# New landing times, DMA rates and matmul steps in the recorder that orders a two-layer GLA and differential-attention trunk

## The chip, the core and the metric

The kernel runs on one core of a Trainium2 chip. Each engine works through its own queue of instructions in order: PE (matmuls, with its weight loads shown as PEld), DVE and ACT (element-wise work), POOL (GpSimd) and SP, whose queue here issues all DMAs. The metric is device time in microseconds (us) of one execution; smaller is better.

## The reference

Two layers over 2048 tokens of width 1024, float32. Each layer normalises and modulates its input, makes one combined projection (width 3600), runs two groups of heads on it, and projects the result back into the residual:

```python
h = rms_norm(x, norm_g[l]) * (1.0 + scale) + shift        # scale, shift, gate from c @ w_ada
gq, gk, gv, glr, gz, dq, dk, dv, dz = split_columns(h @ w_in[l])
# group A, 4 heads: gated linear attention by chunks of 64, state read at the chunk's end
# group B, 4 heads: differential attention, two softmax maps of dh 64, values of 128
p = softmax(where(key_chunk <= query_chunk, q @ k.T, -inf))
attn = p[map 0] - lam * p[map 1]
o_diff = rms_norm(attn @ v) * (1 - lam_init) * silu(dz)
x = x + gate * (concat(o_gla, o_diff) @ w_out[l])
```

## The kernel before

The tokens are worked on in four units of 512 (`u` = 0 to 3), in both layers (`l`). Dense projections are split into a high and a low part in fp32r, three 512-wide matmuls for each 128x128 block (`acc<-w,hhi`, `acc<-w,hlo`, and `oh`, `ol` for the output projection). Weights split in this way are kept in DRAM (`wd`) and loaded again for later units into four buffers `w` of 512 KB.

Attention of a unit and head works by query tiles of 128 (`qt`). For each of the two maps, matmuls make the scores (`sc<-Kj,qh` and `ql`, `Kj` from earlier units and `Kt` from this one); DVE takes the running minimum of the negated scores while it copies them into a score tile `s`, ACT takes the exponential. There are five `s` tiles. POOL first fills a corner of each new one with a mask value (`MEMSET s`). DVE then makes the difference of the two maps. The product with the values needs the weights turned. For most heads (88 query tiles in all, called turned) this goes partly through DRAM: DVE transposes 32x32 blocks (`turn_blocks`), a DMA writes them (`ad<-s`), another reads them back in turned order by pieces of 64 elements (`s<-ad`), and the product `po<-Vj,s` reads that; the tile's own unit is turned on PE (`tp<-ident,s`) and comes in through `po<-Vt,s`. After the product ACT sums squares, POOL takes a power (`wq`), DVE scales by it and the gate (`z`), and PE transposes `z` for the output projection (`to_oT`).

Nothing is issued as it is written. Python generators (`run_streams`) for attention, GLA, dense work and so on take turns by a virtual clock; each instruction is recorded by `Program.record` with its cost (`Program.cost`), its dependencies and its buffers. In `pv`, `WAIT` is how much later on that clock, beyond the arithmetic, the product of a turned query tile may be recorded. `Program.order` then lists the instructions anew: engine by engine, it picks the recorded instruction that is ready, with the lowest turn, by its own table of costs and of latencies from one engine to another (`LAT`; row `S` is the landing of a DMA as seen by ACT, DVE, POOL, PE and another DMA). For the DMA queue it counts 1150 ns from the issue, bytes by a rate, and at most eight in flight. `best_order` repeats that sixty times with changed turns and keeps the order with the shortest span by its own table. `issue` puts the instructions out in that order from one line, which is why the profile shows all work at L370. The table decides only the order; on the chip each engine waits on semaphores.

Of the kernel before, what the change touches and what calls it, by code (L numbers as in the profile page):

```python
# [22 lines left out]
P = 128  # L23
# [97 lines left out]
class Program:  # L121
# [2 lines left out]

    LAT = {"A": dict(A=142, V=141, G=159, T=260, S=84), "V": dict(A=128, V=127, G=155, T=202, S=20),
           "G": dict(A=150, V=100, G=340, T=203, S=17), "T": dict(A=197, V=196, G=200, T=0, S=200),
           "S": dict(A=930, V=930, G=1650, T=1300, S=1700)}

    def __init__(self, **engines):
        self.ops = []  # L130
# [44 lines left out]
    @staticmethod  # L175
    def cost(e, method, args, kw, out):
        n = math.prod(out.shape[1:])
        if e == "S":
            return math.prod(out.shape) * 4 / (256.0 if out.shape[-1] == 64 else 360.0)
        if e == "T":  # L180
            if method == "transpose":
                return 110
            rate = {F32R: 2.4, BF16: 2.4, F32: 0.6}[args[2].dt]
            if rate == 0.6 and args[1].shape[1] < P:
                return 54 if args[1].shape[0] == CH else 60
            return max(n * 0.444, 112 * args[1].shape[1] / P) if rate == 2.4 else max(n / rate, 216) + 6
        ins = [a for a in list(args[1:]) + list(kw.values()) if isinstance(a, View) and a is not kw.get("accum_out")]
        scalars = sum(math.prod(a.shape[1:]) == 1 for a in ins) if n > 1 else 0
        psum = any(a.buf.psum for a in ins)
        half = 112 if out.shape[0] <= 64 and n > 16 else 0  # L190
        if method == "tensor_reduce":
            n = math.prod(ins[0].shape[1:])
        if e == "A":
            return 0.834 * n + (45 if psum else 85) + 93 * (scalars + ("accum_out" in kw)) + half
        if e == "G":
            return 300 + 165 * n if kw.get("op") == ALU.pow else 100 + 2.2 * n
        fast = method in ("tensor_copy", "tensor_scalar") and not psum
        return (0.52 if fast else 1.042) * n + 70 + 61 * scalars + half + 30 * ("accum_out" in kw)
# [175 lines left out]
def trunk_kernel(ctx, tc, x, c, w_ada, b_ada, norm_g, w_in, conv_w, w_gk, b_gk, gla_norm_g,  # L374
# [3 lines left out]
    S = x.shape[1]  # L378
# [22 lines left out]
    V, A, G, T, SY = (prog.queue(e) for e in "VAGTS")  # L401
# [210 lines left out]
    def pe(cost, wait=0.0):  # L612
        return ("pe", cost, wait)
# [434 lines left out]
        HD[key, hd, "q"] = (qh, ql, Kt, Vt, sz)  # L1048
        done("qkT", key, hd)

    WAIT, AFTER = 7.0, 0.0

    def attn_gen(l, u, hd):
        y = layers[l]
# [321 lines left out]
```

## Time and profile before

| | |
|---|---|
| time, median of 3 runs | 2473.82 us (2470.57 to 2479.25) |
| the profiled execution | 2474.07 us, span 2472.4 us |
| instructions | 39660 |
| PE busy | 2408.5 us, 97% |
| DVE, ACT, POOL busy | 1778.4, 1289.0, 138.2 us |
| DMA moved | 568.33 MB, mean 230 GB/s |
| mean granted PE clock | 0.997 |

A profile row names an engine, an operation and its tiles as out<-in, without the numbers of buffers; a wait is put down to what ended it.

### The profile page before, as it was taken

The page shows a single profiled execution, that of the slowest core. Times are in us where ns is not written, and L with a number is a line of the kernel's source. Part 1 is how long each engine was busy: PE and PEld are TensorE (multiplying, and loading weights), DVE is VectorE, ACT ScalarE, POOL GpSimd, SP SyncE. Part 2 cuts the span into 40 slices and gives each one's busy share as a digit, 9 for nine tenths or more (in the row PEclk, how much of TensorE's full clock was granted, in tenths as well). Part 3 has the DMA queues.
Part 4 walks back from the last instruction along what each step waited for, and adds up shares of the span by engine and source line. Part 5 has one row for each costly group of instructions (what it writes and reads, how often), then busy time and mean ns, then how long its engine had stood idle before and what let it go on. Part 6 is the DMA issues. An engine that isn't in the chain of part 4 may idle for free.

```text
span 2472.4 us, 39660 instructions
## 1 busy us (share of the span) xinstructions
PE 2408.5 (97%) x13251; PEld 1962.4 (79%) x13251; DVE 1778.4 (72%) x5169; ACT 1289.0 (52%) x2912; POOL 138.2 (6%) x424
## 2 busy tenths in 40 slices
PE   7999999999999999899999999999999999999999
PEld 5887777787888878787788877888888887878887
DVE  4879777882878828688864895668728887287883
ACT  5757544562555624454773574456614566144552
POOL 0001000010000000000000010000000000000000
PEclk9999999999999999999999999999999999999999
DMA  8777887676686866678457867676677777676763
GB/s 266 275 245 273 310 275 237 215 254 213 216 249 193 278 227 193 195 223 228 143 208 272 283 251 276 207 231 204 201 250 233 229 224 238 213 221 184 233 200 129
DMA packets 425996, 568.33 MB, mean 230 GB/s; under 512 B 195968, under 2 KB 300608, under 8 KB 425792
## 3 DMA queue, kind: packets, MB, share of 16 engines
q1 hardware_dynamic: 425792, 565.79, 70.7%
q8 instruction: 105, 1.72, 0.3%
q14 instruction: 99, 0.81, 0.1%
HBM read 410.52 MB, written 161.48 MB: 231 GB/s over the span
## 4 chain that ended last, share of the span: by engine, by line
PE 43%; DMA 4%; DVE 4%; ACT 1%; issue 1%; SPq 0%; POOL 0%; POOLq 0%; DVEq 0%; ACTq 0%
PE acc L370 29%; PE sc L370 6%; PE po L370 5%; PE tp L370 3%; DVE s L370 2%; DMA ad<-s 2%; DMA s<-ad 1%; DMA w<-wd 1%; SPq L370 0%; DMA wr<-in_w_ada_dram 0%; ACT s L370 0%; DMA xt<-xd 0%; POOL wq L370 0%; DVE w L370 0%; DVE z L370 0%
## 5 line engine op out<-in xcount | busy, mean ns | idle before, releaser
L370 PE MATMUL acc<-w,hhi 128*128 128x512 f32 x2560 | 836.1, 401 | 5.4 <-DMA w<-wd 3.5
L370 PEld LDWEIGHTS acc<-w,hhi 128*128 128x128 f32 x2560 | 466.3, 189 | 97.6 <-DMA w<-wd 7.0
L370 PE MATMUL acc<-w,hlo 128*128 128x512 f32 x1280 | 506.4, 396 | 0.0
L370 ACT ACTIVATE s<-s,mx 128x512 f32<-128x512 f32 (+15 forms) x256 | 308.0, 1204 | 249.6 <-DVE s L370 145.6
L370 PE MATMUL acc<-hhi,w 128*128 128x512 f32 x1024 | 352.1, 398 | 1.4 <-DVE z L370 1.4
L370 PE MATMUL acc<-w,oh 128*128 128x512 f32 x1024 | 333.6, 400 | 3.7 <-ACT oh L370 1.6
L370 DVE TENSOR_SCALAR_CACHE_REDUCE s<-sc,mx 64x64 f32<-64x64 f32 (+5 forms) x640 | 307.1, 483 | 31.1 <-PE sc L370 12.9
L370 PEld LDWEIGHTS acc<-w,hlo 128*128 128x128 f32 x1280 | 240.9, 188 | 49.0 <-issue 1.3
L370 PEld LDWEIGHTS acc<-w,oh 128*128 128x128 f32 x1024 | 189.2, 189 | 44.7 <-DVE t L370 3.6
L370 PEld LDWEIGHTS acc<-hhi,w 128*128 128x128 f32 x1024 | 191.8, 188 | 39.4 <-PE tp L370 1.9
L370 PE MATMUL po<-Vj,s 128*128 128x128 f32 x1536 | 201.7, 283 | 12.7 <-DMA s<-ad 11.4
L370 PEld LDWEIGHTS po<-Vj,s 128*128 128x128 f32 x1536 | 193.4, 197 | 23.9 <-DMA s<-ad 17.8
L370 PE MATMUL acc<-w,ol 128*128 128x512 f32 x512 | 202.3, 398 | 0.0
L370 PE MATMUL acc<-hlo,w 128*128 128x512 f32 x512 | 201.1, 393 | 0.0
L370 DVE SCALAR_TENSOR_TENSOR s<-s,r 128x512 f32<-128x512 f32 (+2 forms) x320 | 198.5, 666 | 2.5
L370 DVE TENSOR_SCALAR_CACHE_REDUCE s<-sc 128x512 f32<-128x512 f32 (+4 forms) x256 | 158.5, 621 | 42.6 <-PE sc L370 38.1
L370 ACT COPY rw<-acc 128x256 f32<-128x256 f32 x128 | 48.0, 375 | 237.2 <-PE acc L370 236.9
L370 PE MATMUL sc<-Kj,qh 128*128 128x512 f32 x384 | 160.4, 418 | 1.0 <-DVE ol L370 0.6
L370 POOL MEMSET s<- 64x64 f32 x256 | 38.5, 151 | 2058.1 <-PE po L370 1384.7
L370 PE MATMUL sc<-Kj,ql 128*128 128x512 f32 x384 | 153.0, 398 | 0.0
L370 ACT CAST w<-raw 128x512 fp32r<-128x512 f32 x152 | 93.2, 626 | 109.0 <-PE acc L370 92.7
L370 DVE TENSOR_TENSOR w<-raw,w 128x512 fp32r<-128x512 f32 x152 | 103.3, 686 | 61.0 <-ACT w L370 60.1
(185 smaller groups left out, 3738.3 us busy)
## 6 DMA issues: line engine op xcount, KB each, us to landing
w<-wd SPq DMA_DIRECT2D x424, 512.0 KB, 4.4
wd<-w SPq DMA_DIRECT2D x144, 512.0 KB, 4.0
raw<-in_w_in_dram SPq DMA_DIRECT2D x120, 256.0 KB, 4.6
Kj<-kd SPq DMA_DIRECT2D x48, 512.0 KB, 5.7
ad<-s SPq DMA_DIRECT2D x24, 768.0 KB, 4.7
s<-ad SPq DMA_DIRECT2D x24, 768.0 KB, 5.9
wr<-in_w_ada_dram SPq DMA_DIRECT2D x128, 128.0 KB, 3.6
ad<-s SPq DMA_DIRECT2D x32, 512.0 KB, 3.7
```

What stands on the lines that cost most here:

```text
L370: getattr(self.engines[e], method)(*[real(a) for a in args], **{k: real(v) for k, v in kw.items()})
```

## The change

Three places of numbers are changed; no instruction is added or left out. The landing of a DMA (row `S` of `LAT`) counts 250 to 700 ns more. The DMA rate, in bytes per ns, is now taken by the size of the last dimension: 208 instead of 256 for 64, 326 instead of 360 for 256, 350 instead of 360 for all others. The steps of matmuls are 0.4485 ns an element instead of 0.444 in fp32r, and 8 or 18 ns of surcharge instead of 6 in float32, the larger one where the stationary operand is a view of more than one step. `WAIT` is 9.0 instead of 7.0.

```diff
-           "S": dict(A=930, V=930, G=1650, T=1300, S=1700)}
+           "S": dict(A=1500, V=1500, G=1900, T=2000, S=2200)}
...
         if e == "S":
-            return math.prod(out.shape) * 4 / (256.0 if out.shape[-1] == 64 else 360.0)
+            return math.prod(out.shape) * 4 / {64: 208.0, 256: 326.0}.get(out.shape[-1], 350.0)
...
-            return max(n * 0.444, 112 * args[1].shape[1] / P) if rate == 2.4 else max(n / rate, 216) + 6
+            if rate == 0.6:
+                return max(n / rate, 216) + (18 if len(args[1].path) > 1 else 8)
+            return max(n * 0.4485, 112 * args[1].shape[1] / P)
...
-    WAIT, AFTER = 7.0, 0.0
+    WAIT, AFTER = 9.0, 0.0
```

The order moves on every engine, mostly by a few places. Three places follow.

On PE in layer 0, fourth unit, first head, ahead of the product of the third query tile (`s_9812` is the tile that comes back from DRAM, `hhi` and `hlo` the input of a projection, `rw` and `z` are other heads' transposes). Before:

```order
L370 MATMUL acc_10531<-w_10597,hhi_9578 128x512 x2
L370 MATMUL acc_10531<-w_10597,hlo_9595 128x512
L370 MATMUL tp_10819<-ident_101,z_10141 128x128 x2
L370 MATMUL tp_10828<-ident_101,s_10567 128x128 x4
L370 MATMUL po_10839<-Vt_10134,s_10724 128x128 x4
L370 MATMUL po_10787<-Vj_9114,s_9812 128x128 x4
L370 MATMUL po_10787<-Vj_9717,s_9812 128x128 x4
L370 MATMUL po_10787<-Vj_9800,s_9812 128x128 x4
```

Now, with that tile as `s_9837`:

```order
L372 MATMUL po_10842<-Vt_10133,s_10699 128x128 x3
L372 MATMUL acc_10859<-w_10758,hhi_9343 128x512 x2
L372 MATMUL acc_10859<-w_10758,hlo_9355 128x512
L372 MATMUL acc_10859<-w_10763,hhi_9348 128x512 x2
L372 MATMUL acc_10859<-w_10763,hlo_9363 128x512
L372 MATMUL acc_10877<-w_10758,hhi_9343 128x512 x2
L372 MATMUL acc_10877<-w_10758,hlo_9355 128x512
L372 MATMUL acc_10877<-w_10763,hhi_9348 128x512 x2
L372 MATMUL acc_10877<-w_10763,hlo_9363 128x512
L372 MATMUL po_10760<-Vj_9130,s_9837 128x128 x4
L372 MATMUL po_10760<-Vj_9768,s_9837 128x128 x4
```

Before, ten short matmuls stood between the last projection matmul and the product; now the tile's own part (`Vt`) is earlier, and twelve projection matmuls follow it.

On SP, the round trip of the same query tile (`ad3_2` in DRAM, `kd` and `vp` keys and values of earlier units). Before:

```order
L370 DMA Kj_10691<-kd0_1_1355 128x1024
L370 DMA w_10698<-wd0_2_1_1776 128x1024
L370 DMA Kj_10711<-kd1_1_4778 128x1024
L370 DMA Kj_10717<-kd2_1_7836 128x1024
L370 DMA ad3_2_10777<-s_10528 128x6x256
L370 DMA w_10805<-wd0_2_2_1833 128x1024
L370 DMA w_10814<-wd0_2_3_1855 128x1024
L370 DMA s_9812<-ad3_2_10777 128x24x64
L370 DMA Vj_10846<-vp0_1_1253 128x512
L370 DMA ad3_3_10851<-s_10724 128x6x256
L370 DMA s_10567<-ad3_3_10851 128x24x64
```

Now:

```order
L372 DMA Kj_10679<-kd0_1_1355 128x1024
L372 DMA Kj_10702<-kd1_1_4776 128x1024
L372 DMA Kj_10727<-kd2_1_7801 128x1024
L372 DMA ad3_2_10753<-s_10517 128x6x256
L372 DMA w_10758<-wd0_2_0_1770 128x1024
L372 DMA w_10763<-wd0_2_1_1776 128x1024
L372 DMA s_9837<-ad3_2_10753 128x24x64
L372 DMA w_10815<-wd0_2_2_1832 128x1024
L372 DMA w_10825<-wd0_2_3_1855 128x1024
L372 DMA ad3_3_10855<-s_10699 128x6x256
L372 DMA Vj_10864<-vp0_1_1252 128x512
```

The write stands two weight loads earlier in the queue: those of the first two pieces of the next item now follow it.

On PE at the end of that unit, where the transposes of `z` wait for the third query tile of the third head (`s_11748` before, `s_11751` now). Before:

```order
L370 MATMUL po_12274<-Vj_11741,s_11748 128x128 x4
L370 MATMUL acc_12237<-w_12310,hhi_9499 128x512
L370 MATMUL acc_12237<-w_12310,hlo_9524 128x512
L370 MATMUL acc_12265<-w_12299,hhi_9494 128x512 x2
L370 MATMUL acc_12265<-w_12299,hlo_9507 128x512
L370 MATMUL tp_12439<-ident_101,z_11186 128x128 x2
L370 MATMUL sc_12445<-Kj_12215,qh_12349 128x512
L370 MATMUL sc_12445<-Kj_12215,ql_12383 128x512
L370 MATMUL acc_12265<-w_12310,hhi_9499 128x512 x2
L370 MATMUL acc_12265<-w_12310,hlo_9524 128x512
L370 MATMUL acc_12286<-w_12299,hhi_9494 128x512 x2
L370 MATMUL tp_12439<-ident_101,z_11186 128x128
```

Now:

```order
L372 MATMUL acc_12083<-w_12316,hhi_9465 128x512 x2
L372 MATMUL acc_12083<-w_12316,hlo_9477 128x512
L372 MATMUL acc_12231<-w_12306,hhi_9457 128x512 x2
L372 MATMUL acc_12231<-w_12306,hlo_9472 128x512
L372 MATMUL acc_12231<-w_12316,hhi_9465 128x512 x2
L372 MATMUL acc_12231<-w_12316,hlo_9477 128x512
L372 MATMUL acc_12267<-w_12306,hhi_9457 128x512 x2
L372 MATMUL acc_12267<-w_12306,hlo_9472 128x512
L372 MATMUL acc_12267<-w_12316,hhi_9465 128x512 x2
L372 MATMUL acc_12267<-w_12316,hlo_9477 128x512
L372 MATMUL tp_12449<-ident_101,z_11190 128x128 x3
```

Before, two of the transposes stood ahead of the third, with twelve 512-wide matmuls between the product and the last; now all three stand together, behind eighteen, of which the rows show fifteen.

## Prediction

> **What bounds the kernel now.** I read the page first, then the waits of PE, the timeline of PE and of the DMA-issuing queue around the longest waits, and the granted clock in stretches around them. The page's first lines:
>
> ```profile
> span 2472.4 us, 39660 instructions
> PE 2408.5 (97%) x13251; PEld 1962.4 (79%) x13251; DVE 1778.4 (72%) x5169; ACT 1289.0 (52%) x2912; POOL 138.2 (6%) x424
> ```
>
> PE is busy for all but 2472.4 - 2408.5 = 63.9 us. No instruction is added or removed by the change, so what PE must do stays; what an order can win lies in those 63.9 us, and in the time that matmuls run at a lower clock. PE's waits, largest first (engine and tile that waited, what ended the wait, us in total, times, longest us):
>
> ```profile
> PE po L370 <- DMA s<-ad: 11.4, 10, 4.8
> PE tp L370 <- DVE z L370: 8.1, 8, 4.0
> PE tp L370 <- DMA wr<-in_w_ada_dram: 5.3, 3, 4.0
> PE tp L370 <- DVE s L370: 4.0, 6, 2.1
> PE acc L370 <- DMA w<-wd: 3.5, 4, 2.0
> ```
>
> The largest is the one that the change speaks of: the attention product (po) waits for the second half of the round trip through DRAM (s<-ad) that turns the attention weights. The fifth is the load of the projections' weights. The third lies at the very start, before there is other work, and the order of the first thirty DMA issues is nearly the same in both orders: it stays. The longest wait of all, in the timeline of PE (start, busy us, what, idle before it and its releaser):
>
> ```profile
> 980.65 0.34 PE L370 MATMUL sc<-Kt,ql 128*128 128x384 f32 x1
> ...
> 1000.45 1.16 PE L370 MATMUL po<-Vt,s 128*128 128x128 f32 x8 [0.67 <-ACT s L370]
> 1006.44 4.42 PE L370 MATMUL po<-Vj,s 128*128 128x128 f32 x24 [4.83 <-DMA s<-ad]
> ```
>
> The query tile's last score matmul starts at 980.65, and its product at 1006.44. Between them the queue that issues the DMAs did this:
>
> ```profile
> 994.54 0.37 SPq L370 DMA_DIRECT2D ad<-s  x1
> 997.49 1.01 SPq L370 DMA_DIRECT2D w<-wd  x2
> 998.61 0.37 SPq L370 DMA_DIRECT2D s<-ad  x1
> 1001.64 2.90 SPq L370 DMA_DIRECT2D Vj<-vp  x1
> ```
>
> The read was issued at 998.61 and released PE at about 1006.4, some 7.8 us later. The typical times from issue to landing, and what the granted clock did in 10 us around the long waits (PE, PEld, DVE, ACT, POOL busy, clock, DMA share, GB/s):
>
> ```profile
> w<-wd SPq DMA_DIRECT2D x424, 512.0 KB, 4.4
> ad<-s SPq DMA_DIRECT2D x24, 768.0 KB, 4.7
> s<-ad SPq DMA_DIRECT2D x24, 768.0 KB, 5.9
> ```
>
> ```profile
> 1002.00:1012.00 10.00, 5.05 (x29) 4.81 (x30) 5.15 (x20) 1.10 (x5) 0.59 (x3) 0.83 0.84 221
> 1165.00:1175.00 10.00, 5.96 (x21) 4.49 (x21) 5.29 (x15) 1.24 (x2) 1.53 (x4) 0.83 0.76 213
> 1202.00:1212.00 10.00, 8.09 (x33) 4.99 (x32) 8.69 (x23) 4.50 (x10) 1.76 (x4) 0.83 0.75 265
> 2189.00:2199.00 10.00, 8.03 (x33) 6.34 (x32) 9.64 (x26) 3.34 (x5) 0.00 (x0) 0.83 1.11 303
> 2437.00:2447.00 10.00, 8.28 (x41) 6.61 (x39) 3.23 (x6) 1.94 (x5) 0.55 (x1) 0.83 0.23 81
> 2216.00:2226.00 10.00, 7.45 (x49) 6.44 (x48) 7.58 (x27) 2.71 (x11) 0.70 (x3) 1.00 0.84 245
> ```
>
> Five stretches have a clock of 0.83, so each loses 0.17 x 10 = 1.7 us of matmul time on top of its idle time; 8.5 us in all.
>
> **The change, part by part.** The recorder's table says when it believes a DMA has landed; it never made PE wait, semaphores do. The old table, for a 768 KB read of 64-element pieces: 1.15 us of issue, 786432 B / 256 = 3.07 us, 1.30 us to PE, 5.5 us in all, against the 5.9 us of the row. The new one: 1.15 + 786432 / 208 = 3.78 + 2.00 = 6.9 us. For the weights, 524288 / 360 = 1.46 gave 3.9 us against 4.4 us, and now 1.50 + 3.15 = 4.6 us. So the old one promised data about half a microsecond early, the new one late by 1.0 and 0.2 us. The matmul steps are the smaller edit: 0.444 x 512 = 227 ns becomes 230 ns, and this row has
>
> ```profile
> 1792.00:1854.00 62.00, 62.00 (x282) 51.39 (x281) 18.09 (x55) 11.96 (x29) 0.00 (x0) 1.00 0.71 249
> ```
>
> 62 us / 282 = 220 ns for a mixture with shorter ones; a step 1% longer in the table moves nothing by itself, and I price it at nothing, with no cover at stake. WAIT 9 instead of 7 lets attention's product stand 2 us later in the order's starting point. In the order as built, I counted for each of the 88 turned query tiles the PE instructions between the tile's last score matmul and its product, each 512-wide matmul at 0.23 us and the others at their own steps: 19.3 us on average before, 21.2 us now. I call this the cover. Now term by term.
>
> *The waits for s<-ad, 11.4 us.* Of the ten, these four have the rows that matter (with the one above):
>
> ```profile
> 2219.11 0.62 PE L370 MATMUL po<-Vj,s 128*128 128x128 f32 x3 [1.71 <-DMA s<-ad]
> 2231.56 0.62 PE L370 MATMUL po<-Vj,s 128*128 128x128 f32 x3 [0.33 <-DMA s<-ad]
> 2266.15 0.62 PE L370 MATMUL po<-Vj,s 128*128 128x128 f32 x3 [0.59 <-DMA s<-ad]
> 444.02 0.74 PE L370 MATMUL po<-Vj,s 128*128 128x128 f32 x4 [1.24 <-DMA s<-ad]
> 494.23 0.62 PE L370 MATMUL po<-Vj,s 128*128 128x128 f32 x3 [0.92 <-DMA s<-ad]
> ```
>
> At 1006.44 the cover has 37 projection matmuls before and 65 now: 28 x 0.23 = 6.4 us more, against a wait of 4.83. At 2219 it is 45 and 66, 4.8 us more against 1.71; at 2231 and 2266 it grows by 6.6 and 7.1 us. These four, 4.83 + 1.71 + 0.33 + 0.59 = 7.5 us, go. At 444 the cover grows by 1.0 (0.2 us stays); at 494 it shrinks by 1.5 (0.92 becomes 2.4); the other four small ones change by little. So the six others keep their 3.9 us. Two query tiles whose products started without any wait lose cover:
>
> ```profile
> 1611.59 0.62 PE L370 MATMUL po<-Vj,s 128*128 128x128 f32 x3
> 2053.25 0.62 PE L370 MATMUL po<-Vj,s 128*128 128x128 f32 x4
> ```
>
> They lose 2.5 and 3.4 us. If their DMAs are issued as late as before, that is up to 5.4 us of new waits (the second has some half a microsecond to spare); if the order issues them earlier too, as the later landings in its table demand, nothing. I take half, 2.7. The term: -7.5 + 2.7 = -4.8 us, bounds -11.4 and +1.
>
> *The weights, 3.5 us in four waits*, of which one is most:
>
> ```profile
> 2192.45 0.51 PE L370 MATMUL acc<-w,hhi 128*128 128x512 f32 x1 [1.97 <-DMA w<-wd]
> ```
>
> PE work from the release of the buffer to the first use: 2.7 us before, 4.2 now, so 1.97 becomes 0.5; the three others gain 1.8 to 3.9 us of cover and go. But ten loads now have under 5.5 us, where six had. -2.5 us, bounds -3.5 and 0.
>
> *A wait on DVE that is a DMA's.* The 4.04 us of the second row:
>
> ```profile
> 1169.49 0.33 PE L370 MATMUL tp<-ident,z 128*128 128x128 f32 x1 [4.04 <-DVE z L370]
> ```
>
> ```profile
> 1167.58 0.14 POOL L370 MEMSET s<- 64x64 f32 x1 [5.29 <-DMA ad<-s]
> ```
>
> The chain: POOL's queue held a memset of a score tile until the write ad<-s had left its buffer, and behind it on POOL stood the power (wq) that DVE's z needs, which PE transposes. Cover from the product to the transposes: 3.1 us before, 5.4 now (the third place of the order above). 2.1 us go, 1.9 stay, since on POOL a memset that waits for a DMA still stands ahead of the power. Bounds -4.0 and 0.
>
> *The clock.* Of five slow stretches, those of 1006 and 2192 rest on waits that go: 2 x 1.7 = 3.4 us, bounds 0 and -5.1. Rows first: the stretch of 2189 lost its clock after a single idle time of 1.97 us, and that of 2216 with 1.71 us did not. The Trainium skill, TensorE: Matmul & The Clock Gate, section "HAM oscillation — how this bites in real kernels", has the rule that idle gaps over about 3.4 us are to be avoided. By that rule only the gaps of 4.83 and 4.04 us would cost clock here, and the term would be 1.7 us; the rows show more stretches than that, so the rows decide.
>
> *All other waits* (63.9 - 11.4 - 3.5 - 4.0 = 45 us, the start's included) rest on durations that the change leaves alone. Their covers move both ways: 2.1 us more at one transpose of scores, 1.5 to 2 us less at some first score matmuls. 0, bounds -6 and +6.
>
> The sum: -4.8 - 2.5 - 2.1 - 3.4 = -12.8 us. The profiled execution took 2474.07 us (1.7 us around its span), and the median of the runs shown is 2473.82: the same. 2474 - 13 = 2461.
>
> **The rivals.** *Waits move, none go (about 2470).* The table has one landing time whatever else is in flight. In the 2189 row DMA stands at 303 GB/s and a share of 1.11; at 1001.64 one issue took the queue 2.90 us. If a late landing is a matter of load, then a fixed 0.7 us more helps the median, not the ten worst: at 1006.44 the read took 7.8 us, over the new table's 6.9 too. Then only the four big covers count, 7.5 us, and new waits of 5.4 us stand against them, with one slow stretch gone: 2474 - 7.5 + 5.4 - 1.7 = 2470. For it: the covers lost above. Against it: the ones gained are larger than any landing seen. The Trainium skill, DMA: Bandwidth & Descriptors, section "Latency and other measured facts", says that HBM access takes 0.2 us on average and 2 us at high load; 7.8 against a median of 5.9 us agrees in direction. That the order doesn't change is excluded: on every engine nearly all rows differ.
>
> *Attention is squeezed (slower).* Later products hold the five score tiles longer, and those are scarce:
>
> ```profile
> POOL s L370 <- PE po L370: 1384.7, 172, 91.5
> ```
>
> The memset that opens a score tile waits for a product to free it nearly all the time. Counted in PE work, the end of the third unit's last head moves back by 10.8 us, the end of the fourth unit's first head by 11.1, and that of its second by -2.5: between the last two stand 68.8 us of PE work where 82.4 stood. In layer 1 it is 68.8 for 81.0. If that head needs its old time, because a tile is free only when the round trip is over, PE runs dry for up to 13.6 + 12.2 = 26 us. Half of it, with nothing won elsewhere: 2474 + 13 = 2487. It decides once the head cannot be done in less than about 75 us. Against it: the covers inside that head grow (the 2266 row is its first query tile), so the order has found room.
>
> **How the numbers follow.** The forecast, waits for DMAs go and the rest stays, gets 0.56, "waits move" 0.25, "squeezed" 0.19. The runs shown spread by 0.3%, so 7.4 us is about what can be told from no change: 2461 is beyond it, 2470 within, 2487 beyond on the other side; so 0.56, 0.25 and 0.19. The forecast's own range: all terms at their better ends -11.4 - 3.5 - 4.0 - 5.1 = -24 us gives 2450, and the near end is 2466. For eight in ten I go up through the second rival and part of the third, to 2482.
>
> **What would show it.** Right: the row "po <- DMA s<-ad" under 6 us, the query tile of 1006 without a long wait, three slow stretches or fewer, the total of PE's idle time under 55 us. Wrong: that row still above 9 us with other query tiles in it; or idle time of PE between the first and second head of the fourth unit, released by DVE or ACT, which would be the squeeze; or a new wait for w<-wd as long as those won.

## The result and the profile after

The changed kernel takes 2454.41 us (median of 4 runs, 2454.02 to 2458.22) against 2475.05 us (4 runs, 2470.57 to 2479.25): a ratio of 0.992, with a 95% interval of 0.990 to 0.9941. It is faster by 0.8%, 20.6 us, where 13 us were forecast, and lies inside the stated range.

The profiled executions stand at 2454.26 and 2474.07 us, 19.8 us apart. The page of the changed kernel begins:

```profile
span 2452.5 us, 39647 instructions
PE 2403.7 (98%) x13251; PEld 1957.3 (80%) x13251; DVE 1778.8 (73%) x5169; ACT 1283.8 (52%) x2912; POOL 138.2 (6%) x424
```

PE's idle time is 2452.5 - 2403.7 = 48.8 us, 15.1 us less than the 63.9 of before, and its busy time is 4.8 us less for the same instructions. The two make the 19.9 us of the span. PE's waits now, in the same view as before (what waited, what ended it, us, times, longest):

```profile
PE tp L372 <- DMA wr<-in_w_ada_dram: 5.1, 2, 4.1
PE tp L372 <- DVE s L372: 3.9, 8, 1.3
PE tp L372 <- DVE z L372: 2.7, 5, 1.6
PE po L372 <- DMA s<-ad: 2.5, 3, 1.1
...
PE acc L372 <- DMA w<-wd: 1.3, 3, 0.7
```

The wait for the round trip fell from 11.4 to 2.5 us, that for the weights from 3.5 to 1.3, that for z from 8.1 to 2.7; the load at the start stayed. Together 16.5 us less, where 15.1 us of idle time were won. The query tile that waited 4.83 us before, in PE's timeline:

```profile
972.36 0.33 PE L372 MATMUL sc<-Kt,ql 128*128 128x384 f32 x1
...
998.18 0.39 PE L372 MATMUL acc<-w,hlo 128*128 128x512 f32 x1
998.41 2.98 PE L372 MATMUL po<-Vj,s 128*128 128x128 f32 x24
```

and its round trip on SP:

```profile
985.51 0.37 SPq L372 DMA_DIRECT2D ad<-s  x1
985.97 2.47 SPq L372 DMA_DIRECT2D w<-wd  x2
990.13 0.37 SPq L372 DMA_DIRECT2D s<-ad  x1
```

From the last score matmul to the product it takes 998.41 - 972.36 = 26.0 us, as much as before (1006.44 - 980.65 = 25.8), and the read is issued 17.8 us after that matmul (18.0 before). So the product did not come sooner after its scores; PE works on projections in the meantime, 65 of their matmuls where it had 37. The clock, in 10 us around the same five places:

```profile
993.00:1003.00 10.00, 9.74 (x62) 8.79 (x63) 7.58 (x27) 3.26 (x11) 0.79 (x3) 1.00 0.89 262
1155.00:1165.00 10.00, 9.32 (x57) 8.03 (x55) 9.86 (x31) 6.18 (x13) 0.38 (x2) 1.00 0.95 241
1190.00:1200.00 10.00, 8.51 (x59) 7.33 (x58) 7.35 (x21) 9.98 (x26) 0.71 (x3) 1.00 0.00 0
2170.00:2180.00 10.00, 8.76 (x41) 6.27 (x41) 9.90 (x28) 4.15 (x8) 0.69 (x1) 1.00 1.00 322
2418.00:2428.00 10.00, 7.58 (x46) 6.38 (x46) 3.59 (x6) 1.97 (x6) 0.55 (x1) 1.00 0.07 27
```

All stand at 1.00 where they stood at 0.83, and the whole span has 1.000 where it had 0.997:

```profile
core 0: 2452.5 us, clock 1.000
```

Five times 1.7 us of clock, 8.5 us, are back. Since busy time fell by only 4.8 us, some 3.7 us of it must have been added elsewhere; no view here shows where. The clock is not an accident of the one profiled execution: all four executions of the change have 0.999 or 1.000, and the executions of the kernel before that ran beside the experiments lie at 0.993 to 0.998.

### The profile page after: what moved, and what is told of

Its sections match the earlier page's. It is cut to its first block, busy times and chain, and to the rows that moved or that the text cites. A ratio compares the mean times of both kernels' runs of the same rounds, so it can differ in the third digit from the quotient of the medians.

```text
span 2452.5 us, 39647 instructions
## 1 busy us (share of the span) xinstructions
PE 2403.7 (98%) x13251; PEld 1957.3 (80%) x13251; DVE 1778.8 (73%) x5169; ACT 1283.8 (52%) x2912; POOL 138.2 (6%) x424
## 5 line engine op out<-in xcount | busy, mean ns | idle before, releaser
L372 ACT ACTIVATE s<-s,mx 128x128 f32<-128x128 f32 (+15 forms) x256 | 308.2, 1204 | 263.3 <-DVE s L372 151.2
L372 PEld LDWEIGHTS acc<-w,hlo 128*128 128x128 f32 x1280 | 240.7, 188 | 48.8 <-issue 0.8
```

The lines of the kernel that those rows point to most:

```text
L372: getattr(self.engines[e], method)(*[real(a) for a in args], **{k: real(v) for k, v in kw.items()})
```

## The experiments

The change has four parts: the landings (row `S`), the rates, the matmul steps and WAIT. Theory 1, after the prediction: the order was built on DMAs landing too early, and the new landings and rates are the cause. Theory 2: WAIT is, since it moves the starting order. Theory 3: luck; any other order moves the time by as much.

### Each part alone

`lat_only`:

```diff
-           "S": dict(A=930, V=930, G=1650, T=1300, S=1700)}
+           "S": dict(A=1500, V=1500, G=1900, T=2000, S=2200)}
```

> Only the landings (row S of the table) are the new ones; rates, matmul steps and WAIT are those of before. Theory 1 (the landings are the cause: the order was built on data promised half a microsecond early): half or more of the 20.6 us, so 2459 to 2465 us, with the row po <- DMA s<-ad at 3 to 6 us (11.4 before) and two slow-clock stretches or fewer (five before). Theory 2 (WAIT is the cause: the starting order sets the cover): 2470 to 2478 us, the row above 9 us. Theory 3 (luck: any other order moves the time by some ten microseconds): anywhere from 2455 to 2485 us, with no relation to that row. The cover counted in its order is 20.4 us on average against 19.3 before and 20.9 of the change.

`rate_only`:

```diff
-            return math.prod(out.shape) * 4 / (256.0 if out.shape[-1] == 64 else 360.0)
+            return math.prod(out.shape) * 4 / {64: 208.0, 256: 326.0}.get(out.shape[-1], 350.0)
```

> Only the DMA rates are the new ones. A 768 KB round-trip read counts 0.7 us more, a 512 KB load of weights 0.04 us more. Theory 1: a third of the gain or less, 2464 to 2472 us, with the row po <- DMA s<-ad at 6 to 9 us and w <- wd at its 3.5 us. Theory 2: 2470 to 2478 us. Theory 3: anywhere from 2455 to 2485 us. Cover in its order: 19.9 us.

`step_only`:

```diff
-            return max(n * 0.444, 112 * args[1].shape[1] / P) if rate == 2.4 else max(n / rate, 216) + 6
+            if rate == 0.6:
+                return max(n / rate, 216) + (18 if len(args[1].path) > 1 else 8)
+            return max(n * 0.4485, 112 * args[1].shape[1] / P)
```

> Only the matmul steps are the new ones (1% longer 512-wide ones, up to 12 ns more for float32). Theories 1 and 2: no cause, 2470 to 2479 us, the row po <- DMA s<-ad at 9 us or more (the cover in its order is 19.0 us, a little less than before). Theory 3: anywhere from 2455 to 2485 us.

`wait_only`:

```diff
-    WAIT, AFTER = 7.0, 0.0
+    WAIT, AFTER = 9.0, 0.0
```

> Only WAIT is 9 instead of 7. Theory 1: little, 2469 to 2477 us, since the list picks by its own landings whatever the turn; the row po <- DMA s<-ad at 8 us or more. Theory 2: most of the gain, 2456 to 2463 us, with that row under 5 us. Theory 3: anywhere from 2455 to 2485 us. Its order differs from that of before as much as the whole change's does (7.5 places on average), with a cover of 19.8 us.

Measured against the kernel before on the same chip; idle is span less PE busy of the profile, and the row is the total wait of po for s<-ad. These two and the clock come from one profiled execution each, which for `lat_only`, `step_only` and `wait_only` took 4 to 5 us less than the median, so the loss of `step_only` does not show in its columns:

| kernel | median us | ratio, 95% interval | PE idle us | row us | clock |
|---|---|---|---|---|---|
| before | | | 63.9 | 11.4 | 0.997 |
| the change | 2454.41 | 0.992 (0.990 to 0.9941) | 48.8 | 2.5 | 1.000 |
| lat_only | 2462.82 | 0.9956 (0.9941 to 0.997) | 56.7 | 6.3 | 0.999 |
| rate_only | 2468.92 | 0.9976 (0.9966 to 0.9985) | 60.2 | 6.8 | 0.996 |
| step_only | 2481.93 | 1.0034 (1.0018 to 1.0049) | 63.2 | 11.3 | 0.998 |
| wait_only | 2470.89 | 0.9989 (0.9978 to 1.0) | 57.3 | 6.3 | 0.998 |

The landings alone give 0.44%, about half of the change, the rates 0.24%, WAIT 0.11% with an interval that reaches 1. These are the times that theory 1 expects (the row of `lat_only` stays just above its 3 to 6 us, and `lat_only` has one slow-clock stretch, where two or fewer were expected), and WAIT falls well short of what theory 2 wanted. Three things fit neither: WAIT nearly halves the row too, to 6.3 us where theory 1 wanted 8 or more; the rates cut the wait for w<-wd from 3.5 to 0.7 us, where it was to stay; and the steps, priced at nothing, lose 0.34%, beyond the 2479 us that was allowed for them.

### Other starts of the search

`before_seed1`, `before_seed2`, and the same edit in the changed kernel as `after_seed1`, `after_seed2`:

```diff
-        ops, rnd = self.ops, random.Random(0)
+        ops, rnd = self.ops, random.Random(1)
```

> The kernel before with another start of the random numbers in the search of orders (1 instead of 0); all tables as before. It asks how far the search by itself moves the time. A fifth of PE's instructions stand elsewhere, by 1.2 places on average. Theory 1 (the landings): 2470 to 2482 us, the row po <- DMA s<-ad at 8 us or more. Theory 3 (luck of the search): the spread over starts is as large as the change, so that this could be as fast as 2460 us.

> As before_seed1 with start 2: theory 1 2470 to 2482 us; theory 3 as fast as 2460 us.

> The changed kernel with another start of the random numbers (1 instead of 0). Theory 1: 2450 to 2462 us, the row po <- DMA s<-ad under 5 us. Theory 3: anywhere up to 2475 us, overlapping with the starts of before.

> As after_seed1 with start 2: theory 1 2450 to 2462 us; theory 3 up to 2475 us.

| kernel | median us | ratio, 95% interval | PE idle us | row us | clock |
|---|---|---|---|---|---|
| before_seed1 | 2476.24 | 1.0008 (0.9996 to 1.0019) | 66.4 | 11.6 | 0.994 |
| before_seed2 | 2474.97 | 1.0011 (0.9998 to 1.0023) | 64.3 | 9.3 | 0.996 |
| after_seed1 | 2458.25 | 0.9933 (0.9912 to 0.9953) | 52.8 | 2.6 | 0.999 |
| after_seed2 | 2462.33 | 0.9953 (0.9937 to 0.9969) | 52.3 | 0.9 | 0.998 |

The old numbers give 1.0000 to 1.0011 over three starts, the new ones 0.992 to 0.9953, and the groups do not meet. So theory 3 falls as far as the search's own chance goes. It may explain a part of the size: the start that the change has is the best of the three, though its interval overlaps with those of the others, and the middle one is 0.9933, some 16 us. But another start moves the order little: a fifth of PE's instructions, by 1.2 places on average, where `wait_only` and the whole change move it by some 7.5 places. An order that differs from the old one by that much with the old numbers kept was not tried, so the luck of one order against another stays a rival for the size of the gain.

### Parts together

`dma_parts` is landings and rates without steps and WAIT, `after_no_step` the change with the old steps, `after_no_wait` the change with WAIT 7, `after_later` the change with landings later still:

```diff
-           "S": dict(A=1500, V=1500, G=1900, T=2000, S=2200)}
+           "S": dict(A=2200, V=2200, G=2600, T=3000, S=2900)}
```

> Landings and rates of the change together, matmul steps and WAIT of before. Alone they gave ratios of 0.9956 and 0.9976. Theory 1 (the DMA's numbers are the cause): 0.990 to 0.995, 2450 to 2463 us, the row po <- DMA s<-ad under 5 us. Rival (the parts only work together, WAIT and steps included): no better than the landings alone, 0.995 to 0.998.

> The change without its matmul steps: landings, rates and WAIT. Alone the steps gave 1.0034. If that loss is the steps' own (a cost table that leads the order astray), this is faster than the change by 4 to 8 us: a ratio of 0.986 to 0.990. If it is the accident of one order, as the three starts of the search suggest (they spread by 0.3%), it lies within 0.3% of the change: 0.989 to 0.995.

> The change without WAIT: landings, rates and matmul steps. Theory 1: within 0.3% of the change, 0.990 to 0.996, the row po <- DMA s<-ad under 5 us. Rival (WAIT carries what the landings don't): 0.996 or more, that row over 6 us.

> The change with landings that lie further beyond the measured ones: PE's 3000 ns instead of 2000, the others' 700 more. If every us of cover helps, the waits for DMAs shrink from 3.8 to under 2 us and the time by some 2 us: 0.990 to 0.992. If a landing that is too late costs elsewhere (score tiles held longer, waits on DVE and ACT instead), it is slower than the change: 0.993 to 0.998.

| kernel | median us | ratio, 95% interval | PE idle us | row us | clock |
|---|---|---|---|---|---|
| dma_parts | 2480.33 | 1.0018 (1.0007 to 1.0028) | 67.6 | 3.5 | 0.997 |
| after_no_step | 2465.17 | 0.9956 (0.9939 to 0.9973) | 60.7 | 0.4 | 0.996 |
| after_no_wait | 2471.59 | 0.9986 (0.9975 to 0.9997) | 57.7 | 4.0 | 0.996 |
| after_later | 2478.73 | 1.0012 (1.0002 to 1.0022) | 61.0 | none | 0.996 |

Here theory 1 falls in the form that it had. In all four the row went as it says, to 4.0 us or less, and in `after_later` the wait is not there at all. Yet landings and rates together, which gave 0.44% and 0.24% alone, are slower than before, and so is the change with later landings. Three of the four times lie outside every range that was expected for them (`dma_parts`, `after_no_step`, `after_later`); `after_no_wait` has the time that the rival wanted and the row that theory 1 wanted. The waits of `dma_parts` on PE:

```profile
PE sc L370 <- DVE s L370: 10.6, 19, 1.6
PE tp L370 <- DVE la L370: 7.9, 3, 3.1
PE acc L370 <- DVE z L370: 6.3, 7, 2.1
...
PE acc L370 <- DVE t L370: 4.2, 4, 1.5
PE po L370 <- DMA s<-ad: 3.5, 2, 2.0
```

The same four kinds of waits on DVE in the changed kernel:

```profile
PE sc L372 <- DVE s L372: 2.5, 5, 0.9
...
PE acc L372 <- DVE t L372: 2.2, 4, 0.9
...
PE tp L372 <- DVE la L372: 1.3, 1, 1.3
...
PE acc L372 <- DVE z L372: 1.2, 3, 0.6
```

29.0 us against 7.2 (and 7.1 in the kernel before): these 21.8 us are more than the difference of idle time, 67.6 - 48.8 = 18.8 us. So what the DMAs no longer hold up waits for DVE now. The prediction had rivals near to this, but neither is it: one had new waits for s<-ad at other query tiles, the other PE idle between two heads of the fourth unit. One of these waits, the one for `la` at the end of the third unit in the first layer, in PE's timeline of `dma_parts`:

```profile
875.82 0.87 PE L370 MATMUL po<-Vj,s 128*128 128x128 f32 x6
879.59 0.62 PE L370 MATMUL tp<-la,chk 128*32 128x256 f32 x2 [2.90 <-DVE la L370]
```

and the stretches around it and its counterpart in the second layer, first of `dma_parts`, then of the change:

```profile
870.00:890.00 20.00, 17.03 (x79) 11.81 (x78) 10.17 (x23) 10.31 (x16) 0.69 (x2) 0.91 0.45 122
2085.00:2105.00 20.00, 16.63 (x79) 11.83 (x78) 8.30 (x16) 10.34 (x17) 0.69 (x2) 0.91 0.43 118
```

```profile
860.00:880.00 20.00, 17.12 (x98) 12.45 (x97) 10.78 (x24) 11.14 (x21) 1.76 (x5) 1.00 0.61 160
2065.00:2085.00 20.00, 18.30 (x104) 13.44 (x103) 9.11 (x18) 11.50 (x22) 1.76 (x5) 1.00 0.63 161
```

Here PE stands behind the chain of the GLA gate: three steps of ACT on `la`, with a load of its function table (1.28 us) before the last, then DVE. DMA is not short there, at shares of 0.43 and 0.45. The idle time also costs clock, (1 - 0.91) x 20 = 1.8 us in each layer, which the changed kernel does not lose.

What follows: later landings or lower rates in the table take PE's waits for DMAs away, in every order that was tried. Summed over all rows that end in a DMA, the loads at the start included, they are 20.1 to 25.7 us in the five profiles with the old landings and rates, and 10.5 to 16.2 us in the nine others. Whether the time falls as well depends on the waits for DVE and ACT and on the clock, and that is not additive: the rows that end in DVE or ACT sum to 33 us before and 30 in the change, but to 48 in `dma_parts` and 44 in `after_no_step` and `after_later`. Taking WAIT out of the change loses 0.7%, where WAIT by itself gave 0.1%. Taking the steps out loses 0.4% instead of winning what they lost alone; but 0.9956 lies beside the 0.9953 that the whole change gives with another start, so that may be the search's chance. The 1% between `dma_parts` and the change is three times the spread of the starts. Why WAIT, perhaps with the steps, is needed in company stays open: the runs show that without it 8.9 us of idle time and a lower clock (0.996) return, not which numbers prevent it. So it is shown that later landings and lower rates remove waits for DMAs; that they are the cause of the gain in time is not. No version's ratio lies below that of the change.

## Why the prediction was right, point by point

**The sign, and the kind of time that was won, were right.** What the prediction named as signs came: the row at 2.5 us (under 6), the query tile of 1006 without a wait, no slow stretch (three or fewer), 48.8 us of idle time (under 55). The terms sum to 12.8 us; the profiles differ by 19.8. The idle time that was won is that of the three terms on waits, 8.9 + 2.2 + 4.0 = 15.1 us, and the rest is PE's busy time. The prediction read its covers in the finished order, so it did not need to know which edit made them. As an account of causes it was less right: it priced the steps at nothing and gave WAIT no term, while its reasons are the landings and rates, and those two without steps and WAIT gain nothing (`dma_parts`, 1.0018).

**The waits for s<-ad**, -4.8 forecast, -8.9 measured. The four that were to go are gone. What was mis-sized is the 3.9 us of the six others, which were to stay: all six are gone as well. At the query tile of 494.23 the wait was even to grow to 2.4 us, because its cover shrank by 1.5; now its product starts without idle time:

```profile
485.89 0.87 PE L372 MATMUL po<-Vj,s 128*128 128x128 f32 x6
```

The 2.7 us of new waits came out at 2.5 us, but by luck. Neither of the two query tiles that were to wait does; three others do that did not before:

```profile
868.29 0.97 PE L372 MATMUL po<-Vj,s 128*128 128x128 f32 x6 [1.09 <-DMA s<-ad]
1124.28 0.97 PE L372 MATMUL po<-Vj,s 128*128 128x128 f32 x6 [0.48 <-DMA s<-ad]
2073.42 0.85 PE L372 MATMUL po<-Vj,s 128*128 128x128 f32 x5 [0.95 <-DMA s<-ad]
```

The cover is only half of a race: the order moves the producers too. One of the two named query tiles, before:

```profile
1593.10 0.40 PE L370 MATMUL sc<-Kt,ql 128*128 128x512 f32 x1
```

```profile
1606.71 0.39 SPq L370 DMA_DIRECT2D s<-ad  x1
```

and after:

```profile
1575.05 0.39 PE L372 MATMUL sc<-Kt,ql 128*128 128x512 f32 x1
...
1590.74 0.51 PE L372 MATMUL po<-Vj,s 128*128 128x128 f32 x3
```

```profile
1584.83 0.37 SPq L372 DMA_DIRECT2D s<-ad  x1
```

The read is issued 9.8 us after the last score matmul instead of 13.6, and the product starts without idle time although its cover shrank by 2.5 us. For these two the lower end of the price, nothing, was the right one. The average cover, 21.2 us in the prediction, is 20.9 when only matmuls of queries count as a tile's last score; 19.3 before holds.

**The weights**, -2.5 forecast, -2.2 measured. The sum is near, its parts less so: the wait of 1.97 us went whole, where 0.5 was to stay, and three waits of 0.68, 0.25 and 0.42 us stand at other places, where none was to be left.

**The wait on z**, -2.1 forecast. At that place all 4.0 us went, and the reason given for 1.9 us to stay was wrong. POOL after:

```profile
1144.04 0.14 POOL L372 MEMSET s<- 64x64 f32 x1 [10.16 <-PE po L372]
1144.91 0.55 POOL L372 TENSOR_TENSOR wq<-oss,mhalf 128x1 f32<-128x1 f32 x1 [0.73 <-ACT oss L372]
...
1151.25 0.14 POOL L372 MEMSET s<- 64x64 f32 x1 [3.08 <-DMA ad<-s]
```

A memset still stands ahead of the power, but it takes a buffer that a product frees; the one that waits for the write now stands behind it.

**The clock**, -3.4 forecast, -8.5 by the granted clock, the term with the largest error; of this, PE's busy time shows 4.8 us. I let only the two stretches go whose waits were to go, or nearly so. All five went: that of 1165 with its wait; for the other two the length of the idle time is not the reason. In the last one PE still idles for 10 - 7.58 = 2.4 us at a clock of 1.00 (the 2418 row), where before 10 - 8.28 = 1.7 us came with 0.83. A finer look at that place, before (the columns as in the table of the prediction):

```profile
2439.62:2443.03 3.41, 1.69 (x8) 0.93 (x7) 1.10 (x2) 1.00 (x3) 0.55 (x1) 1.00 0.44 154
2443.03:2446.45 3.42, 3.42 (x10) 2.64 (x9) 1.97 (x3) 0.00 (x0) 0.00 (x0) 0.50 0.06 21
```

and after:

```profile
2418.63:2422.04 3.41, 2.23 (x21) 1.99 (x19) 0.00 (x0) 1.25 (x4) 0.53 (x1) 1.00 0.00 0
2422.04:2425.45 3.41, 2.17 (x9) 1.66 (x10) 1.46 (x3) 0.69 (x1) 0.02 (x1) 1.00 0.01 2
```

In the trace before, each of the five slow stretches is one piece of 3.41 us at half clock, which makes the 1.7 us. The five pieces lie whole multiples of that (3.413 us) apart, and in the piece ahead of each PE was busy for 0.00, 0.37, 1.80, 1.44 and 1.69 us. At this place the idle time of before falls into one piece, that of after is shared by two, and both keep 2.17 us or more of work. So what counts is how the idle time falls on these pieces, and the prediction counted it by waits.

**All other waits**, 0 forecast, 0 measured: 63.9 - 11.4 - 3.5 - 4.0 = 45.0 us before, 48.8 - 2.5 - 1.3 = 45.0 us now. In this sum the other waits of the row of z fell by 1.4 us, and the rest rose by as much.

**The rivals.** "Waits move" did not decide for this change. In `dma_parts` and `after_later` waits did move and the gain was lost, but to DVE and ACT and not, as the rival had it, to other query tiles. The squeeze did not come. The last transposes of `z` of the fourth unit's first and second head in layer 0, before and after:

```profile
1020.52 0.33 PE L370 MATMUL tp<-ident,z 128*128 128x128 f32 x1
...
1103.93 0.27 PE L370 MATMUL tp<-ident,z 128*128 128x128 f32 x1
```

```profile
1018.01 0.28 PE L372 MATMUL tp<-ident,z 128*128 128x128 f32 x1
...
1088.27 0.33 PE L372 MATMUL tp<-ident,z 128*128 128x128 f32 x1
```

From one to the other it takes 70.3 us where it took 83.4, close to the 68.8 and 82.4 us of PE work that the prediction counted, and under the 75 us from which the rival would have decided. The head had slack.

## What to carry to other kernels

When a table orders the work, look at PE's waits by what ended them: those ended by a DMA, apart from the loads at the very start, are where the table's landings can be wrong, and they fell in every order built here with later landings or lower rates. Then look at what the same order does to the other waits and to the clock, because there the gain can be lost whole: landings and rates together cut the wait for the round trip from 11.4 to 3.5 us and were slower by 0.2%. Run a few starts of the search beside such a change; here they spread by 0.1% with the old table and by 0.3% with the new one, which is the least that the order's luck can be worth.

## What the runs showed of the hardware

The read of 768 KB took longer, by its median from issue to landing, in the orders that waited least for it. The rows of `s<-ad`, of the change and of `after_later`:

```profile
s<-ad SPq DMA_DIRECT2D x24, 768.0 KB, 7.4
```

```profile
s<-ad SPq DMA_DIRECT2D x24, 768.0 KB, 9.0
```

Before it was 5.9 us. In the seven profiles where po waited 6.3 us or more for it in all, the median lies at 5.6 to 6.1 us; in the three where po waited 2.6 us or less and a median is given, at 6.4, 7.4 and 9.0 us. So a landing "as measured on the chip" is a property of an order, not of the transfer alone: with the table at 6.9 us the median went to 7.4 and po waited 2.5 us in all. Why it grew was not tried.

A single idle time of 1.97 us (at 2192) cost 1.7 us of clock before, one of 1.71 us (at 2219) did not. The first lies whole in one of the pieces of 3.41 us, and PE was busy for 1.44 us of that piece; the second falls on two, with 3.05 and 2.06 us of work:

```profile
2190.45:2193.86 3.41, 1.44 (x9) 1.25 (x9) 3.35 (x9) 1.58 (x3) 0.00 (x0) 1.00 1.02 322
2193.86:2197.28 3.42, 3.42 (x11) 2.74 (x11) 3.16 (x11) 1.60 (x3) 0.00 (x0) 0.50 1.11 340
```

The border is not sharp. In the fourteen traces, cut into such pieces and without the first 26 us, every piece with less than 1.5 us of PE work was followed by one at half clock, and no piece at full clock with more than 2.25 us was; between the two, either happened. The Trainium skill, TensorE: Matmul & The Clock Gate, section "HAM oscillation — how this bites in real kernels", puts the harm at gaps over about 3.4 us; the rows here disagree. (By that rule the prediction's term for the clock would have been 3.4 us and not the 1.7 that it gives: of its gaps of 4.83 and 4.04 us, nothing and 1.9 us were to be left.)
